# Two-layer hybrid decoder step: the MLP's down product in Strassen-Winograd form on a window of operands that moves, and low parts of weights by an accumulating DMA

## Chip, cores and metric

One NeuronCore of a Trainium2 chip runs the whole step in one launch. The metric is the device time of that launch in microseconds (us), the median of several runs.

## What is computed (the reference, cut)

Two layers over 1024 prompt tokens and 8 x 4 sample tokens, 1056 columns T in all, in fp32. The change is in the last three lines of a layer:

```python
for l in range(DEPTH):
    h = rms_norm(x, attn_norm[l])
    mix, nk, nv, ns = mixer(h, ...)          # window attention beside the HGRN2 recurrence
    x = x + jnp.einsum('ble,ed->bld', mix, w_o[l])
    h = rms_norm(x, mlp_norm[l])
    u = jnp.square(jax.nn.relu(jnp.einsum('bld,df->blf', h, w_up[l])))      # 1024 -> 4096
    x = x + jnp.einsum('blf,fd->bld', u, w_down[l])                         # 4096 -> 1024
return rms_norm(x, final_norm), ...
```

## The kernel before, in words

Activations lie transposed, features on the 128 partitions and tokens along a row. The tokens are split in `HALF` 0 (512 columns) and `HALF` 1 (544). An fp32 product is made of three matmuls in the fp32r type: each operand is split in a high part (a rounded copy) and a low part (the operand minus its high part), and `part` issues high x high, low x high and high x low into one PSUM bank. For weights `Weights.split` makes the parts: ACT copies the raw tile `wraw` into `whi`, DVE subtracts into `wlo`, 512 columns at a time; six tiles of each kind rotate. SP loads `wraw` (512 KB each, three rotate).

The up product is already in Strassen-Winograd form. Two row blocks of the weight (a pair, 16 pairs per layer) and two column blocks of the tokens of a half make a 2x2 block product that needs 7 products, not 8. `WINO` names the 7 pieces: of the weight A11, S3, S2, A12, S1, S4, A22 (the S are sums that DVE makes in place in `wraw`, or in `ws`), of the tokens B11, T3, T2, B21, T1, B22, T4. The token operands stay in SBUF for the stage, four tiles per piece and half (`x0B`, `x0T`, `x1B`, `x1T` in the traces, with high and low part in one tile). For each piece and half PE issues 4 x 3 matmuls of 256 or 272 columns; `up` then combines the 7 results out of PSUM into four blocks of u (`u11` to `u22`), which go to DRAM (`ud`).

The down product is plain: `load_u` brings a block of 128 rows of u back (`ur`), scales it by `rstd`, applies relu and square and splits it into `uh`, `ul`; `down(g)` adds four such blocks into the residual `xT`, for each of 8 output blocks, in chunks of 512, 272 and 272 columns. The last group of layer 0 loads its weights twice, to finish half 0 first; the last group of layer 1 splits its weights ahead (`split_last`), and `after` normalises as blocks end.

No engine's order is written by hand. Every operation becomes an `Op` with a modelled cost and a priority (the model's clock plus `slack[0]`), and the planner emits each engine's operations in the order that the model gives; each engine then runs its own list in that order, waiting on semaphores. PE's list comes from the generators (`up`, `down`), which yield while no PSUM bank is free in the model. PSUM has 8 banks: two of `acc`, four of `mx`, and one each for `aops` and `hops`, where the second piece's result (i = 1) of a half waits for the third.

The order of the pieces in time is:

```python
steps = [(0, h, i) for h, i in [(0, i) for i in range(6)] + [(1, 0), (1, 1), (1, 2), (0, 6)] + [
    (1, i) for i in range(3, 7)]]
steps += [(p, h, i) for p in range(1, pairs) for i in range(7) for h in range(2)]
```

Of the kernel before, what the change touches and what calls it, by code (L numbers as in the profile page):

```python
# [26 lines left out]
F32 = mybir.dt.float32  # L28
# [7 lines left out]
P = 128  # L36
# [18 lines left out]
SUMS = 20.0  # L55
LP = 2
# [14 lines left out]
TAIL = [(0, (0, 512)), (1, (0, 352)), (1, (352, 192))]  # L71
# [3 lines left out]
FG = 4  # L75
# [4 lines left out]
NG = DFF // (P * FG)  # L80
# [6 lines left out]
def tile_hybrid_step(  # L87
# [156 lines left out]

    def cols(x):
        n = 1
        for d in x.shape[1:]:
            n *= d
        return n
# [21 lines left out]
    DQ = Queue(nc.sync, None, 0.0)  # L271
    EN = dict(V=V, S=S, G=G)
# [41 lines left out]
    ud = [dram.tile([DFF // P, P, T], F32, name=f"ud{l}") for l in range(DEPTH)]  # L314
# [97 lines left out]
    class Weights:  # L412
# [4 lines left out]

        def __init__(self):
            self.src, self.raw, self.until, self.units, self.index, self.parts = [], [], [], [], {}, []
            self.last, self.s2 = 1 << 30, None  # L420
# [28 lines left out]
        def split(self, eng):  # L449
# [5 lines left out]
            def two(hi, lo, x):  # L455
                S.activation(out=hi, in_=x, func=AF.Copy)
# [26 lines left out]
        def split_last(self):  # L483
            n = UNIT // FG
            while len(self.parts) < len(self.units):
                r = self.units[len(self.parts)][2][0]
                if len(self.raw) == r:
                    self.load()
                raw, parts = self.raw[r], []
                for o in range(0, UNIT, 512):  # L490
                    hi, lo = (fresh(act.tile([P, 512], F32R, tag="A0", name="wl"), "A0", 16) for _ in range(2))
                    S.activation(out=hi, in_=raw[:, o:o + 512], func=AF.Copy)
                    (V if o else G).tensor_tensor(out=lo, in0=raw[:, o:o + 512], in1=hi.bitcast(F32), op=ALU.subtract)
                    parts += [(hi[:, c:c + n], lo[:, c:c + n]) for c in range(0, 512, n)]
                self.parts.append(parts)

        def reach(self, j, eng=V):
            while len(self.parts) <= min(j, self.last - 1, len(self.units) - 1):
# [105 lines left out]
    for l in range(DEPTH):  # L604
# [694 lines left out]
    def main():  # L1299
        xg, pre, before = [[], []], [], poolR  # L1300
        for l in range(DEPTH):
# [139 lines left out]
            us = {}  # L1441

            def load_u(f):


                tag, bufs, pool = ("A", 16, act) if (f + 8) % 14 < 8 else ("B", 12, poolU)
                us[f] = []
                slack[0] = SLACK
                for h, (base, n) in enumerate(HALF):
                    hi, lo = (fresh(pool.tile([P, n], F32R, tag=f"{tag}{h}", name=f"u{p}", bufs=bufs), f"{tag}{h}", bufs)  # L1450
                              for p in "hl")
                    r = fresh(poolU.tile([P, 544], F32, tag="ts", name="ur", bufs=3), "ts", 3)[:, :n]
                    dma(out=r, in_=ud[l][f, :, base:base + n], after=[ud[l][f, :, base + n // 2:base + n]])
                    V.scalar_tensor_tensor(out=r, in0=r, scalar=0.0, in1=rstd[h], op0=ALU.max, op1=ALU.mult)
                    S.activation(out=r, in_=r, func=AF.Square)
                    S.activation(out=hi, in_=r, func=AF.Copy)
# [258 lines left out]
```

## Time and profile before

| | |
|---|---|
| median of 3 runs | 2452.84 us (2450.91 to 2454.5) |
| profiled execution | 2449.32 us, span 2447.5 us |
| PE busy / DVE / ACT / POOL | 97% / 72% / 43% / 5% |
| mean granted TensorE clock | 0.992 |
| DMA | 256.51 MB, 105 GB/s |
| up stages | about 515 to 858 and 1735 to 2058 us |
| down stages | about 858 to 1229 and 2058 to 2434 us |

The rows below are from one profiled execution. Times are in us from the start of the span unless marked ns. "idle before" is time in which the engine did nothing ahead of an instruction, with what released it. A matmul's duration is longer than its distance to the next, since matmuls are pipelined: distances between starts are what the array takes.

### The profile page before, as it was taken

What the parts mean: (1) busy time and instruction counts of PE and PEld (TensorE: products, weight loads), DVE (VectorE), ACT (ScalarE), POOL (GpSimd) and SP (SyncE); (2) the same over time, 40 slices, a digit from 0 to 9 for tenths busy, and PEclk for the clock granted to TensorE, in tenths of its full rate; (3) what the DMA queues carried; (4) which work ended last, traced back from release to release, by engine and by line L of the source; (5) the groups of instructions that cost most, each with busy time, mean ns of one, the idle gap of its engine ahead of it and who ended that gap; (6) DMA issues with size and microseconds to landing.
All of it is one profiled execution on the core that took longest, in us unless ns stands there. A gap on an engine that the chain in (4) does not pass through costs nothing.

```text
span 2447.5 us, 43079 instructions
## 1 busy us (share of the span) xinstructions
PE 2386.2 (97%) x16752; PEld 2215.6 (91%) x16752; DVE 1768.7 (72%) x3936; ACT 1062.1 (43%) x2170; POOL 126.3 (5%) x120
## 2 busy tenths in 40 slices
PE   8999999989999999999999999999899999999997
PEld 6789998879999989999988899988899999899997
DVE  8988877896666686553688888869866667756436
ACT  6675655642222363231457556546322224523213
POOL 2000001100000000000100000101000000000003
PEclk9999999989999999999999999999999999999999
DMA  5223234423333462221322232353233335423202
GB/s 193 69 87 116 72 105 127 134 73 106 105 105 106 137 184 89 96 88 44 128 98 87 90 125 80 111 155 107 79 102 106 105 105 180 128 92 103 68 27 80
DMA packets 139468, 256.51 MB, mean 105 GB/s; under 512 B 15968, under 2 KB 73184, under 8 KB 139232
## 3 DMA queue, kind: packets, MB, share of 16 engines
q1 hardware_dynamic: 139264, 253.76, 32.0%
q8 instruction: 132, 2.16, 0.4%
q14 instruction: 72, 0.59, 0.1%
HBM read 198.37 MB, written 57.36 MB: 104 GB/s over the span
## 4 chain that ended last, share of the span: by engine, by line
PE 81%; DVE 13%; DMA 3%; ACT 2%; issue 1%; POOL 0%; SPq 0%; DVEq 0%; ACTq 0%
PE acc L347 68%; PE hops L347 3%; PE aops L347 3%; DVE wlo L231 2%; PE lv L347 2%; DMA mixL<-mixd 1%; PE sps L347 1%; PE tps L350 1%; DVE xT L231 1%; DVE z L231 1%; DMA ur<-ud 1%; DVE u L231 1%; DVE ur L231 1%; PE kv L347 1%; DVE ul L231 0%
## 5 line engine op out<-in xcount | busy, mean ns | idle before, releaser
L231 ACT ACTIVATE whi<-wraw 128x512 fp32r<-128x512 f32 x560 | 344.4, 627 | 712.8 <-PE acc L347 562.8
L231 DVE TENSOR_TENSOR wlo<-wraw,whi 128x512 fp32r<-128x512 f32 x560 | 387.0, 706 | 145.4 <-ACT whi L231 136.7
L347 PE MATMUL acc<-ul,whi 128*128 128x272 f32 (+1 forms) x1440 | 464.6, 323 | 2.3 <-DVE ul L231 2.3
L347 PE MATMUL acc<-uh,whi 128*128 128x272 f32 (+1 forms) x1440 | 464.2, 322 | 2.0 <-DVE xT L231 1.3
L347 PE MATMUL acc<-uh,wlo 128*128 128x272 f32 (+1 forms) x1440 | 463.9, 322 | 0.0
L231 DVE TENSOR_TENSOR xT<-xT,acc 128x272 f32<-128x272 f32 (+3 forms) x384 | 198.1, 518 | 261.0 <-PE acc L347 260.5
L347 PEld LDWEIGHTS acc<-uh,whi 128*128 128x128 f32 x1440 | 271.0, 188 | 23.1 <-issue 1.5
L347 PEld LDWEIGHTS acc<-ul,whi 128*128 128x128 f32 x1440 | 270.5, 188 | 22.8 <-DVE ul L231 3.2
L347 PEld LDWEIGHTS acc<-uh,wlo 128*128 128x128 f32 x1440 | 271.3, 188 | 19.7
L347 PE MATMUL acc<-xg1h,whi 128*128 128x272 f32 x704 | 214.5, 305 | 0.0
L347 PE MATMUL acc<-xg1h,wlo 128*128 128x272 f32 x704 | 202.5, 288 | 0.0
L347 PE MATMUL acc<-xg1l,whi 128*128 128x272 f32 x704 | 202.3, 287 | 0.0
L347 PE MATMUL acc<-xg0h,whi 128*128 128x512 f32 x352 | 148.0, 421 | 7.1 <-ACT xg0h L231 5.7
L347 PE MATMUL acc<-x0T,whi 128*128 128x256 f32 x768 | 142.6, 283 | 8.2 <-ACT whi L231 8.2
L347 PE MATMUL acc<-x1B,whi 128*128 128x272 f32 x768 | 148.5, 288 | 0.0
L347 PE MATMUL acc<-x1T,whi 128*128 128x272 f32 x768 | 148.2, 288 | 0.0
L347 PE MATMUL acc<-x0B,whi 128*128 128x256 f32 x768 | 142.7, 284 | 4.4 <-ACT p L231 4.4
L347 PE MATMUL acc<-xg0h,wlo 128*128 128x512 f32 x352 | 140.0, 398 | 4.4 <-DVE wlo L231 4.4
L347 PE MATMUL acc<-xg0l,whi 128*128 128x512 f32 x352 | 139.3, 396 | 1.8 <-DVE xg0l L231 1.8
L347 PEld LDWEIGHTS acc<-xg1h,whi 128*128 128x128 f32 x704 | 132.9, 189 | 3.4 <-issue 2.7
L347 PEld LDWEIGHTS acc<-xg1l,whi 128*128 128x128 f32 x704 | 132.9, 189 | 0.4
L347 PEld LDWEIGHTS acc<-xg1h,wlo 128*128 128x128 f32 x704 | 132.6, 188 | 0.0
(302 smaller groups left out, 5370.7 us busy)
## 6 DMA issues: line engine op xcount, KB each, us to landing
wraw<-win SPq DMA_DIRECT2D x86, 512.0 KB
wraw<-wd SPq DMA_DIRECT2D x68, 512.0 KB
wraw<-wu SPq DMA_DIRECT2D x64, 512.0 KB
ud<-u SPq DMA_DIRECT2D x128, 136.0 KB
ur<-ud SPq DMA_DIRECT2D x64, 272.0 KB
wraw<-wo SPq DMA_DIRECT2D x32, 512.0 KB
ud<-u SPq DMA_DIRECT2D x128, 128.0 KB
ur<-ud SPq DMA_DIRECT2D x64, 256.0 KB
```

The lines of the kernel that those rows point to most:

```text
L231: o = Op(self, ins, outs, lambda: f(*args, **kw), lambda: self.cost(op, outs[0], kw), port=shared)
L347: tensor(t, out, [lhsT, rhs], kw["start"], lambda: TE.matmul(out, lhsT, rhs, **kw))
L350: tensor(0.11, out, [in_], True, lambda: TE.transpose(out, in_, idn))
```

## The change

1. **Down in seven products.** `down` becomes the same `winograd` routine as `up`. A step p (16 per layer) makes one pair of output blocks (pair p % 4, so `xT[m]` and `xT[m+1]` with m = 2(p % 4)) from the four pairs of u blocks p to p + 3 (mod 16); the host lays `wd` out for that. The four are held in the operand tiles of the up stage. After piece i of step p has used its tiles, `load_u` loads the same piece of pair p + 4 into the slot that has come free, so the set moves by one pair a step: 19 pairs of 14 tiles are loaded per layer. Results are added to `xT` straight from PSUM.
2. **u is stored ready.** `up` now applies `rstd`, relu and square (`fin`) and makes the sums T1 to T4 of u before it stores, so `ud` holds 7 pieces of half width in place of 4 quarters, and `load_u` only splits: the DMA lands in the low part's tile, ACT copies the high part, DVE subtracts in place.
3. **Low parts by DMA.** For the pieces S3, A12, S4 of up and A11, S3, S2, A12, S4 of down, DVE's subtraction goes: ACT writes -high into `wlo`, and a DMA that POOL issues adds the raw tile to it (256 in all, 256 KB each). The planner models it as 0.8 us and 5 us more.
4. **Ends.** The sums of squares for the next norm are made as output pairs end, the two column halves of a token half get their `root` apart; `split_last`, the doubled last group, `TAIL` and `after` go.

```diff
+    class Adder(Engine):
+        def take(self, t, d):
+            return t + d, t + d + 5.0
...
+    def dma_add(out, in_):
+        Op(GQ, [in_, out], [out], lambda: nc.gpsimd.dma_start(out=out, in_=in_, accum_op=ALU.add),
+           lambda: 0.8).func = None
...
-    ud = [dram.tile([DFF // P, P, T], F32, name=f"ud{l}") for l in range(DEPTH)]
+    ud = [dram.tile([NPAIR * 7, P, T // 2], F32, name=f"ud{l}") for l in range(DEPTH)]
...
             def two(hi, lo, x):
+                if j in self.adds:
+                    S.activation(out=lo, in_=x, func=AF.Copy, scale=-1.0)
+                    dma_add(lo.bitcast(F32), x)
+                    S.activation(out=hi, in_=x, func=AF.Copy)
+                    return
                 S.activation(out=hi, in_=x, func=AF.Copy)
                 eng.tensor_tensor(out=lo, in0=x, in1=hi.bitcast(F32), op=ALU.subtract)
...
-        def split_last(self):
...
-        for p in range(NG * FG // 2):
+        for p in range(NPAIR):
             W.add_pair((l, "up", p), wu[l, 2 * p], wu[l, 2 * p + 1])
-        for g in range(NG):
-            for rep in range(2 if g == NG - 1 and l < DEPTH - 1 else 1):
-                for u in range(4):
-                    W.add((l, "down", g, rep, u), wd[l, g, u], FG)
-    W.last = W.index[DEPTH - 1, "down", NG - 1, 0, 0]
+        for p in range(NPAIR):
+            W.add_pair((l, "down", p), wd[l, p, 0], wd[l, p, 1])
+    W.adds = {i for k, i in W.index.items() if k[1]=="down" and k[-1] in (0,1,2,3,5) or k[1]=="up" and k[-1] in (1,3,5)}
...
+            def load_u(q, i, h):
+                hi, lo = operand(h, WINO[i][1])[q % 4]
+                r, o = lo.bitcast(F32), 256 * h
+                dma(out=r, in_=ud[l][7 * q + i, :, o:o + HALF[h][1] // 2])
+                S.activation(out=hi, in_=r, func=AF.Copy)
+                V.tensor_tensor(out=lo, in0=r, in1=hi.bitcast(F32), op=ALU.subtract)
...
+            def lead(p):
+                return [(p, h, i) for h, i in [(0, i) for i in range(6)] + [(1, 0), (1, 1), (1, 2), (0, 6)] + [
                     (1, i) for i in range(3, 7)]]
...
+            def winograd(phase, steps, xs, evac):
+                units = [W.index[l, phase, p, i] for p, _, i in steps]
...
+                    while phase == "up" and (i >= 3 and not rstd_ok[h] or i >= 4 and not rstd_ok[1]):
                         yield
                     slack[0] = -URGENT
+                    evac(p, h, i, acc, banks.get((h, 1)))
...
+                    def fin(t):
+                        o, x = (int(t[2]) - 1) * c, tile_(t)
+                        V.scalar_tensor_tensor(out=x, in0=x, scalar=0.0, in1=rstd[h][:, o:o + c], op0=ALU.max, op1=ALU.mult)
+                        S.activation(out=x, in_=x, func=AF.Square)
...
                         add("u12", acc, "u12")
-                        put("u12")
+                        slack[0] = LATER
+                        fin("u12")
+                        less("T3", "u22", "u12")
+                        put(1, "T3")
+                        less("u12", "u12", "u11")
+                        put(4, "u12")
+                        less("T2", "u22", "u12")
+                        put(2, "T2")
...
+                    if p == NPAIR - 1:
+                        slack[0] = SLACK
+                        for q in range(4):
+                            load_u(q, i, h)
+                yield from winograd("up", lead(0) + [(p, h, i) for p in range(1, NPAIR) for i in range(7) for h in range(2)],
...
+            def down():
+                def evac(p, h, i, acc, p7):
+                    base, n = HALF[h]
+                    c, m = n // 2, p % 4 * 2
+                    tile_, add = mine("down", p, h)
+                    def out(f, t, *ys):
+                        x = xT[m + f - 1][h][:, (t - 1) * c:t * c]
+                        for y in ys:
+                            V.tensor_tensor(out=x, in0=x, in1=y, op=ALU.add)
+                    if i == 0:
+                        S.activation(out=tile_("p1"), in_=acc, func=AF.Copy)
+                    elif i == 2:
+                        add("U2", acc, "p1")
+                        add("u21", p7, "U2")
+                    elif i == 3:
+                        out(1, 1, acc, tile_("p1"))
+                    elif i == 4:
+                        add("u12", acc, "U2")
+                        out(2, 2, acc, tile_("u21"))
+                    elif i == 5:
+                        out(1, 2, acc, tile_("u12"))
+                    elif i == 6:
+                        out(2, 1, acc, tile_("u21"))
+                    slack[0] = 3 * SLACK
+                    if p < NPAIR - 1:
+                        load_u((p + 4) % NPAIR, i, h)
...
+                yield from winograd("down", [(p, h, i) for p in range(NPAIR - 1) for i in range(7) for h in range(2)] + lead(
+                    NPAIR - 1), lambda p, h, i: [operand(h, WINO[i][1])[(p + k) % 4] for k in range(4)], evac)
...
+    wd = a["w_down"].reshape(2, 16, 2, 128, 4, 2, 128)
+    wd = np.stack([wd[:, :, :, :, s % 4][:, [(s + k) % 16 for k in range(4)]] for s in range(16)], axis=1)
+    wd = wd.transpose(0, 1, 5, 4, 3, 2, 6).reshape(2, 16, 2, 128, 1024)
```

What stands on DVE, ACT and POOL inside a step of the down stage, before and after. **DVE before**, in the down stage of layer 0 (`ur` to `uh`, `ul` is a block of u, `xT` the residual):

```order
L231 SCALAR_TENSOR_TENSOR ur<-ur,rstd_78 128x512
L231 TENSOR_TENSOR xT_0_4880<-xT_0_4880,acc 128x512
L231 SCALAR_TENSOR_TENSOR ur<-ur,rstd_79 128x544
L231 TENSOR_TENSOR xT_1_4881<-xT_1_4881,acc 128x272
L231 TENSOR_TENSOR ul<-ur,uh 128x512
L231 SCALAR_TENSOR_TENSOR ur<-ur,rstd_78 128x512
L231 TENSOR_TENSOR xT_1_4881<-xT_1_4881,acc 128x272
L231 TENSOR_TENSOR ul<-ur,uh 128x544
```

**DVE after**, from the fourth and fifth piece of a step in the middle of layer 0's down stage; the name in brackets is what the row waits for (DMAHW: an SP transfer, DMASW: a POOL transfer, with its semaphore's number):

```order
L232 TENSOR_TENSOR xT6_0_4892<-xT6_0_4892,acc_13287 128x256 [waits PE_49]
L232 TENSOR_TENSOR x1B21_6205<-x1B21_6205 128x272 [waits DMAHW1_49,Activation_49]
L232 TENSOR_TENSOR xT6_0_4892<-xT6_0_4892,u12_13262 128x256 [waits DVE_49]
L232 TENSOR_TENSOR x0T1_5492<-x0T1_5492 128x256 [waits DMAHW2_49,Activation_49]
L232 TENSOR_TENSOR xT6_1_4893<-xT6_1_4893,acc_13310 128x272 [waits PE_49]
L232 TENSOR_TENSOR wraw_12828<-ws_13242,wraw_12828 128x512 [waits DMASW0_49]
L232 TENSOR_TENSOR xT6_1_4893<-xT6_1_4893,u12_13262 128x272 [waits DVE_49]
L232 TENSOR_TENSOR x1T1_6209<-x1T1_6209 128x272 [waits DMAHW3_49,Activation_49]
L232 TENSOR_TENSOR xT7_0_4894<-xT7_0_4894,acc_13334 128x256 [waits PE_49]
L232 TENSOR_TENSOR wlo_13333<-wraw_12828,whi_13332 128x512 [waits Activation_49]
L232 TENSOR_TENSOR xT7_0_4894<-xT7_0_4894,u21_13183 128x256 [waits DVE_49]
```

The chunks of 512 and 544 columns have become pieces of 256 and 272; `wraw_12828<-ws_13242,wraw_12828` is S1, written over A11, and it waits for the POOL transfer that reads A11. Behind it on DVE stand the additions that free PSUM banks.

**ACT after**, the same step's pieces S3, S2, A12 (`wlo<-` is the negated copy), and **POOL after**, the five transfers of that step and the first of the next:

```order
L232 ACTIVATE wlo_13203<-wraw_13079 128x512 [waits DMAHW6_49,DMASW5_49,DVE_49]
L232 ACTIVATE whi_13202<-wraw_13079 128x512 [waits Activation_49]
L232 ACTIVATE wlo_13241<-ws_13242 128x512 [waits DMASW6_49,DVE_49,PE_49]
L232 ACTIVATE whi_13240<-ws_13242 128x512 [waits Activation_49]
L232 ACTIVATE wlo_13286<-wraw_12828 128x512 [waits DMASW2_49,PE_49]
L232 ACTIVATE whi_13285<-wraw_12828 128x512 [waits Activation_49]
L232 ACTIVATE x1B21_6205<-x1B21_6205 128x272 [waits DMAHW1_49]
L232 ACTIVATE x0T1_5492<-x0T1_5492 128x256 [waits DMAHW2_49]
```

```order
L288 DMA wlo_13162<-wraw_12828 128x512 [waits DMAHW3_49,DMASW4_49,Activation_49]
L288 DMA wlo_13203<-wraw_13079 128x512 [waits DMASW5_49,DMAHW6_49,PE_49,Activation_49]
L288 DMA wlo_13241<-ws_13242 128x512 [waits DMASW6_49,DMASW2_49,Activation_49]
L288 DMA wlo_13286<-wraw_12828 128x512 [waits DMASW3_49,Activation_49]
L288 DMA wlo_13373<-wraw_12828 128x512 [waits PE_49,Activation_49]
L288 DMA wlo_13456<-wraw_13123 128x512 [waits DMAHW3_49,DMASW1_49,Activation_49]
```

POOL had no instruction here before; each of its rows now waits for ACT's negated copy, and the later ones stand behind it in POOL's list.

**DVE after, where up ends**: rows of the last up pair, with loads of down's operands (`x0B`, `x1B`, `x0T`) between the additions of up (`U`, `u`):

```order
L232 TENSOR_TENSOR x0B_5456<-x0B_5456 128x256
L232 TENSOR_TENSOR u_10667<-aops,U_10666 128x256
L232 TENSOR_TENSOR U_10666<-acc,p_10580 128x272
L232 TENSOR_TENSOR x0B_5457<-x0B_5457 128x256
L232 TENSOR_TENSOR u_10667<-hops,U_10666 128x272
L232 TENSOR_TENSOR x0B_5458<-x0B_5458 128x256
L232 TENSOR_TENSOR x1B_5673<-x1B_5673 128x272
L232 TENSOR_TENSOR u_10716<-acc,p_10580 128x256
L232 TENSOR_TENSOR x1B_5674<-x1B_5674 128x272
L232 TENSOR_TENSOR x1B_5675<-x1B_5675 128x272
```

Between the addition `U_10666<-acc,p_10580` of the last up pair and its like in the first down step there are 87 rows on DVE now (82 of 256 or 272 columns, 5 of 512); an ordinary up pair has 38 (25 before), an ordinary down step 42.

## Rows read from the trace of the kernel before

**Rows 1.** The profile's page: the span; busy time, share and instructions of each engine (PE is matmul, PEld weight load); then TensorE's granted clock, in tenths of full speed, in 40 slices of the span.

```profile
span 2447.5 us, 43079 instructions
PE 2386.2 (97%) x16752; PEld 2215.6 (91%) x16752; DVE 1768.7 (72%) x3936; ACT 1062.1 (43%) x2170; POOL 126.3 (5%) x120
...
PEclk9999999989999999999999999999999999999999
```

**Rows 2.** The table of stretches, one line for each stage: up and down of layer 0, then of layer 1. Columns: the stretch in us; its length; busy us and instructions of PE, PEld, DVE, ACT, POOL; granted clock; busy share of the DMA engines; GB/s.

```profile
515.00:858.00 343.00, 335.29 (x2697) 333.53 (x2696) 227.57 (x453) 99.55 (x183) 0.00 (x0) 0.99 0.32 107
858.00:1186.00 328.00, 326.36 (x2032) 297.36 (x2032) 194.21 (x345) 106.75 (x173) 0.00 (x0) 1.00 0.31 96
1735.00:2062.00 327.00, 325.05 (x2639) 323.79 (x2640) 214.55 (x421) 90.92 (x162) 0.00 (x0) 1.00 0.34 113
2062.00:2388.00 326.00, 324.11 (x2021) 295.49 (x2021) 188.77 (x336) 103.76 (x169) 4.23 (x3) 1.00 0.29 90
```

**Rows 3.** The chain of work that ended last, in order of time: start, duration, engine, tile. One link of the up stage is 144 matmuls of one pair of blocks.

```profile
678.93 17.63 PE acc L347 x144
843.41 4.40 PE acc L347 x36
856.89 3.85 DMA ur<-ud
1776.57 17.62 PE acc L347 x144
2043.77 2.96 PE acc L347 x24
```

**Rows 4.** The timeline of PE, single matmuls (start us, duration us, shape): first of the down stage and first of the layer after it; then first and last of the down stage of layer 1.

```profile
857.95 0.40 PE L347 MATMUL acc<-uh,whi 128*128 128x512 f32 x1
1229.00 0.40 PE L347 MATMUL acc<-xg0h,whi 128*128 128x512 f32 x1
2058.29 0.40 PE L347 MATMUL acc<-uh,whi 128*128 128x512 f32 x1
2433.28 0.27 PE L347 MATMUL acc<-uh,wl 128*128 128x192 f32 x1
```

**Rows 5.** The timeline of PE in the up stage: the first of 12 matmuls on 256 columns, the first of the 12 on 272 columns behind them, and the first of the next 256.

```profile
705.22 0.40 PE L347 MATMUL acc<-x0T,whi 128*128 128x256 f32 x2
706.65 0.41 PE L347 MATMUL acc<-x1T,whi 128*128 128x272 f32 x2
708.16 0.40 PE L347 MATMUL acc<-x0B,whi 128*128 128x256 f32 x2
```

**Rows 6.** The timeline of DVE in the up stage, instructions with no idle time between them.

```profile
700.97 0.42 DVE L231 TENSOR_TENSOR U<-acc,p 128x256 f32<-128x256 f32 x1 [0.15 <-PE acc L347]
701.43 0.42 DVE L231 TENSOR_TENSOR u<-aops,U 128x256 f32<-128x256 f32 x1
...
703.31 0.68 DVE L231 TENSOR_TENSOR wlo<-wraw,whi 128x512 fp32r<-128x512 f32 x1
703.91 0.42 DVE L231 TENSOR_TENSOR u<-acc,p 128x256 f32<-128x256 f32 x1
704.26 0.68 DVE L231 TENSOR_TENSOR ws<-wraw 128x512 f32<-128x512 f32 x1
...
708.72 0.43 DVE L231 TENSOR_TENSOR u<-acc,u 128x272 f32<-128x272 f32 x1
709.07 0.68 DVE L231 TENSOR_TENSOR wlo<-wraw,whi 128x512 fp32r<-128x512 f32 x1
```

**Rows 7.** The table of stretches again, inside the up and the down stage of layer 0 away from their ends (columns as in rows 2).

```profile
560.00:800.00 240.00, 240.00 (x1963) 240.00 (x1962) 150.04 (x293) 59.68 (x106) 0.00 (x0) 1.00 0.32 104
870.00:1180.00 310.00, 309.89 (x1938) 283.11 (x1937) 180.80 (x323) 98.99 (x161) 0.00 (x0) 1.00 0.29 92
```

**Rows 8.** The page's part on DMA queues: packets, MB, share of the span of 16 engines.

```profile
q1 hardware_dynamic: 139264, 253.76, 32.0%
```

**Rows 9.** Groups of instructions, shapes kept apart: line, engine, operation, out<-in, count | busy us, mean ns of one | idle before, releaser.

```profile
L231 DVE TENSOR_TENSOR wlo<-wraw,whi 128x512 fp32r<-128x512 f32 x560 | 387.0, 706 | 145.4 <-ACT whi L231 136.7
L231 ACT ACTIVATE whi<-wraw 128x512 fp32r<-128x512 f32 x560 | 344.4, 627 | 712.8 <-PE acc L347 562.8 <-DVE wraw L231 83.9 <-issue 56.0
L231 DVE SCALAR_TENSOR_TENSOR ur<-ur,rstd 128x544 f32<-128x544 f32 x64 | 46.2, 722 | 5.1 <-DMA ur<-ud 4.7
L231 DVE TENSOR_TENSOR u<-acc,u 128x272 f32<-128x272 f32 x96 | 42.1, 438 | 27.1 <-PE acc L347 27.1
L231 DVE TENSOR_TENSOR u<-acc,u 128x256 f32<-128x256 f32 x96 | 40.3, 421 | 5.2
L231 POOL TENSOR_TENSOR u<-u,u 128x512 f32<-128x512 f32 x12 | 16.6, 1385 | 728.6 <-ACT u L231 728.6
L231 ACT ACTIVATE p<-acc 128x256 f32<-128x256 f32 x32 | 12.4, 387 | 28.9 <-PE acc L347 27.1 <-DVE x1T L231 1.9
```

**Rows 10.** The timelines of DVE and POOL after the last down matmul, when both scale the output.

```profile
2434.72 4.64 DVE L231 SCALAR_TENSOR_TENSOR y<-xT,fn_t,rstd 128x352 f32<-128x352 f32 x5
2440.76 2.82 DVE L231 SCALAR_TENSOR_TENSOR y<-xT,fn_t,rstd 128x192 f32<-128x192 f32 x5
2434.73 3.26 POOL L231 TENSOR_TENSOR y<-xT,rstd 128x352 f32<-128x352 f32 x3 [3.40 <-ACT tmp L231]
2440.80 1.91 POOL L231 TENSOR_TENSOR y<-xT,rstd 128x192 f32<-128x192 f32 x3 [2.81 <-DVE rstd L231]
```

**Rows 11.** What writes or reads the scratch tensor `ud` (SPq is SP's DMA queue; issue ns min/median/max), and who waited for it.

```profile
L278 SPq DMA_DIRECT2D ud<-u x256: 319/320/473, 534.1 to 2059.2; - x128
L278 SPq DMA_DIRECT2D ur<-ud x128: 319/320/1347, 839.3 to 2298.3; - x128
...
who waited for it (us, times):
  DVE ur L231: 12.4, 22
```

More of the change, by code (lines that the diff above doesn't have):

```diff
@@ L481, in split @@
             slack[0] = 0.0
-        def split_last(self):
[L484 to L495, printed above, removed]
         def reach(self, j, eng=V):
-            while len(self.parts) <= min(j, self.last - 1, len(self.units) - 1):
+            while len(self.parts) <= min(j, len(self.units) - 1):
                 while len(self.raw) <= self.units[len(self.parts)][2][-1]:
@@ L1439, in main @@
             yield from o_proj(1)
[L1441 to L1456, printed above, removed]
-                    V.tensor_tensor(out=lo, in0=r, in1=hi.bitcast(F32), op=ALU.subtract)
-                    us[f].append((hi, lo))
-                slack[0] = 0.0
@@ L1461, in up @@
-            def up():
-                pairs = NG * FG // 2
-                steps = [(0, h, i) for h, i in [(0, i) for i in range(6)] + [(1, 0), (1, 1), (1, 2), (0, 6)] + [
+            def load_u(q, i, h):
[4 more added lines that the diff above has]
+                V.tensor_tensor(out=lo, in0=r, in1=hi.bitcast(F32), op=ALU.subtract)
@@ L1464, in up @@
+            def lead(p):
+                return [(p, h, i) for h, i in [(0, i) for i in range(6)] + [(1, 0), (1, 1), (1, 2), (0, 6)] + [
                     (1, i) for i in range(3, 7)]]
-                steps += [(p, h, i) for p in range(1, pairs) for i in range(7) for h in range(2)]
-                units = [W.index[l, "up", p, i] for p, _, i in steps]
-                banks, tiles = {}, {}
+            def winograd(phase, steps, xs, evac):
+                units = [W.index[l, phase, p, i] for p, _, i in steps]
+                banks = {}
@@ L1502, in up @@
                         add("U2", acc, "p1")
[L1503 removed]
+                        add("u21", p7, "U2")
                     elif i == 3:
                         add("u11", acc, "p1")
[L1506 removed]
+                        slack[0] = LATER
+                        fin("u11")
+                        put(0, "u11")
                     elif i == 4:
@@ new lines, in main, with square @@
+            ssq, roots = {}, [0, 0]
+            def square(h, m, o, n, last=False):
+                x = xT[m][h][:, o:o + n]
+                if last:
+                    S.activation(out=rstd[h][:, o:o + n], in_=x, func=AF.Square)
+                    spawn(root(h, o, n))
+                elif not m:
+                    rstd_ok[h] = False
+                    ssq[h] = utile("u22" if h else "u11")
+                    S.activation(out=ssq[h][:, o:o + n], in_=x, func=AF.Square)
+                else:
+                    t = fresh(poolU.tile([P, 544], F32, tag="ts", name="sq", bufs=3), "ts", 3)[:, :n]
+                    S.activation(out=t, in_=x, func=AF.Square)
+                    V.tensor_tensor(out=ssq[h][:, o:o + n], in0=ssq[h][:, o:o + n], in1=t, op=ALU.add)
+                if l == DEPTH - 1 and m % 3 == 1:
+                    S.activation(out=x, in_=x, func=AF.Identity, scale=fn_t[:, m:m + 1])
@@ L1592, in main @@
             yield from up()
-            wide[0] = True
-            for g in range(NG):
-                yield from down(g)
-            wide[0] = False
+            yield from down()
             if l < DEPTH - 1:
```

166 lines of the change are left out of this document (78 added, 88 removed).

## The prediction

> **What bounds the kernel now.** I began with the page's busy times: PE works 97% of the span and TensorE's granted clock is at full speed in nearly all 40 slices [rows 1], so time can only come from fewer or cheaper matmuls. The table of stretches says the same by stage: in both up and both down stages PE's busy time is within a few us of the length, save the first 40 us of an up stage, and DVE, the next busiest, is at 58 to 66% [rows 2]. The chain of waits then gives the pace of the up stage, the model for what down is to become: links of a pair of blocks start at 678.93 and, eight pairs later, at 843.41, so a pair takes 20.56 us; in layer 1 it is (2043.77 - 1776.57) / 13 = 20.55 [rows 3]. Single matmuls explain the pace: 12 on 256 columns take 706.65 - 705.22 = 1.43 us and 12 on 272 take 1.51 [rows 5], and 7 x (1.43 + 1.51) = 20.6. No pair of the steady stage waits for anything. The down stage goes from 857.95 to 1229.00 = 371.1 us in layer 0, and from 2058.29 to the end of its last matmul, 2433.55, = 375.3 us in layer 1 [rows 4], 746.4 in all.
>
> **What the seven products take away.** After the change a step of down is the same 7 x 2 x 12 matmuls on the same shapes as a pair of up, with one weight piece for each 24 of them. Were PE never to wait, 32 steps would take 32 x 20.56 = 657.9 us: **88.5 us less**. That is the ceiling; everything that follows takes from it.
>
> **Is DVE still faster than PE?** In a steady up pair DVE's rows go from 25 (11 of 512 columns, 14 of 256 or 272) to 38 (8 and 30), and a down step has 42 (6 and 36). Back to back, a 512 row takes 703.91 - 703.31 = 0.60 us and a 256 row 704.26 - 703.91 = 0.35, a 272 row 709.07 - 708.72 = 0.35; one that needs the result before it takes 701.43 - 700.97 = 0.46 [rows 6]. That gives 8 x 0.60 + 30 x 0.35 = 15.3 us for up and 6 x 0.60 + 36 x 0.35 = 16.2 for down. By the mean durations, which overlap, it would be 30 x 0.43 + 8 x 0.706 = 18.5 and 36 x 0.43 + 6 x 0.706 = 19.7 [rows 9]. Before, 25 rows came to 150.04 us in 240, or 12.85 a pair [rows 7], 1.12 times what the distances give (11.5); with that factor I take 17.1 and 18.1 of 20.56. DVE stays hidden, with 2.5 us to spare in down, and no longer with 8. ACT is far off: in down 12 rows of 512 and 16 small ones, 12 x 0.63 + 16 x 0.39 = 13.8 us [rows 9].
>
> **What the accumulating DMAs cost.** They show nowhere in the trace of before. Their bytes must pass the 16 DMA engines. The main queue moved 253.76 MB in 32.0% of the span, 324 GB/s while busy [rows 8]; 104 GB/s at a share of 0.32 in the up stage says 325 [rows 7]. A down step moves two raw tiles (1.05 MB) and 14 loads (1.89 MB), 2.94 MB or 9.1 us; an up pair as much, with stores for loads. An added tile of 0.26 MB costs 0.8 us if it passes once, 1.6 if source and destination are both read, 2.4 if it passes three times. For five adds that is 13.1, 17.2 or 21.2 us a step. I take the middle, since an add reads two streams where the plain transfers of the row read one: 84% of the step, hidden, but with queues. The upper end is 0.6 us over PE's pace, 20 us in 32 steps. Between 0 and 20 I take **+10** for steady waits of both stages.
>
> The waits that they add stand in order. DVE waits for the transfer of A11 ahead of S1 and for that of A12 ahead of S4, since both sums overwrite what the transfer reads; behind them on DVE stand the additions that free PSUM, and PE waits for these when its banks are full. Six banks of 1.47 us give it some 8 us. SP waits for the adds before it reloads `wraw`, and behind that stand the loads of u; POOL's adds wait for ACT's copy and for each other. Six weight tiles rotate, each for 2.94 us of matmuls, so an add has some 10 us before PE wants it. All this is hidden while an add lands within about 8 us; beyond that each us late is a us for PE, in every step.
>
> The Trainium skill bears on this (SBUF — State Buffer, Who interferes with whom): a DVE instruction with two SBUF inputs and a GpSimd one that reads SBUF exclude each other, while a POOL-issued DMA is starved only by DVE's two-port copies. The trace agrees with the first half: beside POOL's scaling, five 352-column rows of DVE take 4.64 us, 0.93 each, where a 544-column row takes 0.72 alone [rows 9, 10]. By the second half issuing the adds would cost DVE nothing, as in my sum; no run here shows it yet.
>
> **Where up ends.** The four first pairs for down can be loaded only as the last up pair lets go of its tiles. Between the like rows of the two stages DVE has 87 rows, 82 x 0.35 + 5 x 0.60 = 31.7 us against 20.56. SP has 72 transfers there: 56 loads (7.57 MB), 14 stores (1.89), two raw tiles (1.05), 10.5 MB or 32 us, with some eight adds 39 to 45 us, in the 36 us from the first tile let go to the last one wanted. SP's issue time, 72 x 0.32 = 23 us [rows 11], isn't the limit. DVE is 11 us late, and banks and later slack of 2.5 us a step absorb part; DMA is 3 to 9 us late, of the same delay. From 1 to 15 us a layer I take 7, **+14**. Today the same place costs 1 to 3 us, already counted in the 746.4.
>
> **The smaller ends.** In the first up pair `fin` and the differences add 16 rows to DVE (5.6 us) and three subtractions go (1.8), in a stretch where DVE and `rstd` already hold PE; half of it shows: 2 a layer, **+4** (0 to 8). At the end of layer 0 the operands for the next layer need 8 x 0.64 us of DVE, less than the four pieces of half 1 that PE still has (6 us): hidden, **+1** with the tail of layer 1. There the last matmul now ends with two dependent additions, a square, a root and eight scalings of 272 columns in place of 192; before, 13.9 us pass from the last matmul to the end [rows 4, 10], and I expect 12 to 16.
>
> **Sum.** -88.5 + 10 + 14 + 4 + 1 = -59.5. The profiled execution took 2449.32 us, 3.5 below the median 2452.84 of the three runs; from the median the forecast is **2393 us**. With every cost at its lower bound it is 2364, with every one at its upper (20 + 30 + 8 + 4) 2427.
>
> **Rivals.**
> *The adds are slow.* If an add holds all 16 engines longer than (20.56 - 9.1) / 5 = 2.3 us, DMA sets the pace of down, and each us more costs 5 x 32 = 160 us. At 2.67 us the gain is gone; at 3 us the kernel takes about 2500. For it: nothing in the trace bounds an add from above. Against: three passes would be 2.4. The skill's fixed price (DMA: Bandwidth & Descriptors, Anatomy of one DMA: 2.0 us plus bytes at 436 GB/s) makes 2.6 us from issue to landing for 256 KB, by which an add would be early enough; it speaks of plain transfers, and no run here shows one from POOL.
> *POOL's issue blocks DVE.* All DVE rows between SBUF tiles have two inputs. An issue of 0.32 us, like SP's [rows 11], would cost DVE 1.6 us a step and stay hidden; one like a POOL row, 1.39 us [rows 9], would make 18.1 + 6.9 = 25 us. At 0.85 it is 22.3, 1.8 over PE, 57 us in down: about 2450, no change. The skill's rule above speaks against it.
> *DVE's list sets the pace.* With rows that wait for transfers, for ACT and for each other, 18.1 us can become 22: 1.5 x 32 = 46 us, 2439, still faster. For it: the spare is 2.5 us, and DVE runs its list in the planner's order.
>
> **Chances.** The forecast (2364 to 2427) 0.60; DVE's list 0.15; slow adds 0.12; POOL's lock 0.10, half of it slower; the rest 0.03. The range 2364 to 2450 leaves out the slow adds, half of the lock and a little below. About 0.2%, 5 us, is what a measurement here can tell from no change. Faster 0.77, same 0.05, slower 0.18.
>
> **What would show it.** Right: links of 20.56 us in the chain of both down stages; DVE busy some 85% of them; gaps of PE at the first down steps of 5 to 10 us, before matmuls on down's operands, released by DVE or by a load; DMA share about 0.8 in down. Wrong: DVE rows on `wraw` or matmuls on `wlo` that wait for POOL's transfers in every step (slow adds); DVE rows of 0.6 us or more on 256 columns (the lock); steps of 21 to 23 us with DVE never idle (its list); a lower granted clock in down.

## The result, and the profile after

The changed kernel takes 2484.84 us (median of 4 runs, 2479.80 to 2486.59), the kernel before beside it 2452.89: ratio 1.0129, 95% interval 1.0113 to 1.0145. It is 32 us **slower**; the forecast was 2393. The profiled execution took 2479.80 us, its span is 2478.0.

The page of the changed kernel (answers to [rows 1, 8]): span, busy times, granted clock in 40 slices, the two DMA queues that carry data, the group of POOL's issues, and the issue with its median us to landing.

```profile
span 2478.0 us, 49266 instructions
PE 2347.5 (95%) x17534; PEld 2223.2 (90%) x17534; DVE 2007.3 (81%) x5027; ACT 1369.9 (55%) x3106; POOL 330.0 (13%) x361
...
PEclk9999999989999989999999999999899998999998
...
q1 hardware_dynamic: 225472, 314.95, 41.1%
q0 software_dynamic: 36864, 67.13, 15.3%
...
L288 POOL DMA_DIRECT2D wlo<-wraw x224 | 194.6, 880 | 1210.0 <-ACT wlo L232 756.3
...
wlo<-wraw POOLq DMA_DIRECT2D x224, 256.0 KB, 4.5
```

PE works less than before (2347.5 against 2386.2 us) and waits more. DVE is not full. The stretches of the changed kernel (columns as in [rows 2]): up away from its ends, the end of up, the first down step, down away from its ends; then the first down step and the later ones of layer 1.

```profile
600.00:840.00 240.00, 238.83 (x1941) 237.61 (x1940) 186.34 (x439) 107.96 (x231) 30.51 (x35) 1.00 0.66 178
845.00:865.00 20.00, 17.41 (x137) 16.65 (x136) 13.84 (x40) 12.45 (x32) 2.40 (x3) 1.00 0.95 278
865.00:905.00 40.00, 26.88 (x170) 25.73 (x169) 30.50 (x81) 24.64 (x64) 4.52 (x6) 0.79 0.95 259
910.00:1180.00 270.00, 259.47 (x2079) 255.36 (x2078) 206.99 (x519) 151.25 (x347) 53.73 (x62) 1.00 0.82 200
2084.00:2122.00 38.00, 27.07 (x164) 25.72 (x164) 29.79 (x81) 24.05 (x63) 4.33 (x5) 0.78 0.93 257
2125.00:2400.00 275.00, 260.87 (x2063) 255.46 (x2062) 207.53 (x518) 152.62 (x352) 53.03 (x62) 0.99 0.79 191
```

Two things stand out against [rows 7]: the first down step has PE busy for 27 of 40 us, at a granted clock of 0.79 (part of it at 1.2 GHz, behind waits), with the DMA engines at 0.95; and the later steps have PE idle for 10.5 of 270 us while DVE is busy for 77%. The waits of PE in that first step (in brackets: idle before, and what ended it):

```profile
871.54 0.80 PE L357 MATMUL aops<-x0T,whi 128*128 128x256 f32 x2 [3.34 <-ACT whi L232]
876.44 0.58 PE L357 MATMUL aops<-x0T,wlo 128*128 128x256 f32 x1 [4.10 <-DMA wlo<-wraw]
890.65 0.50 PE L357 MATMUL acc<-x0T,whi 128*128 128x256 f32 x2 [3.43 <-ACT whi L232]
...
897.99 0.58 PE L357 MATMUL acc<-x0B,wlo 128*128 128x256 f32 x1 [2.04 <-DMA wlo<-wraw]
```

Two of them are waits for an added tile itself, 6.1 us (6.5 in layer 1). In all later steps of both layers such waits come to 3.1 us.

A pair of up and a step of down are each 168 matmuls, so a step is measured from the first matmul of one to the first of the next, in the profiled execution. The first three boundaries of layer 0's down stage, on PE's timeline (start, duration, shape): steps of 40.24 and 23.91 us.

```profile
865.11 0.40 PE L357 MATMUL acc<-x0B,whi 128*128 128x256 f32 x2
...
905.35 0.50 PE L357 MATMUL acc<-x0B,whi 128*128 128x256 f32 x2
...
929.26 0.40 PE L357 MATMUL acc<-x0B,whi 128*128 128x256 f32 x2
```

All runs in one table, each cell layer 0 / layer 1 in us: mean of pairs 2 to 15 of up; last pair of up and first step of down together (PE alone needs 41.1); mean of steps 3 to 13 of down; the down stage; and the time as a ratio to the kernel before, with its interval; four kernels ran once, and their time stands there instead.

| kernel | up pair | last + first | down step | down stage | ratio |
|---|---|---|---|---|---|
| before | 20.56 / 20.55 | | | 371.1 / 375.3 | 1 |
| changed | 20.79 / 20.81 | 64.4 / 65.8 | 21.77 / 22.37 | 373.5 / 374.3 | 1.0129 (1.0113 to 1.0145) |
| e1 no adds in down | 20.56 / 20.91 | 59.6 / 59.4 | 21.04 / 21.15 | 355.8 / 354.7 | 0.9962 (0.9948 to 0.9975) |
| e2 none in first step | 20.88 / 20.86 | 60.4 / 61.0 | 22.26 / 21.89 | 378.2 / 371.0 | 1.0120 (1.0104 to 1.0136) |
| e3 S4 over A21 | 20.83 / 20.63 | 66.6 / 65.9 | 21.63 / 21.77 | 371.3 / 368.5 | 1.0101 (1.0075 to 1.0126) |
| e4 no adds | 21.00 / 20.99 | 58.3 / 57.0 | 21.16 / 21.19 | 355.9 / 354.8 | 0.9956 (0.9939 to 0.9973) |
| e5 traffic in layer 1 | 20.96 / 20.85 | 61.0 / 69.8 | 21.02 / 22.37 | 356.0 / 376.7 | 2468.09 us, one run |
| e6 two sets | 20.81 / 20.82 | 59.8 / 63.0 | 21.86 / 20.94 | 366.1 / 355.7 | 2455.49 us, one run |
| e7 POOL issues | 21.05 / 20.86 | 60.0 / 59.1 | 21.18 / 20.96 | 353.7 / 348.3 | 0.9968 (0.9958 to 0.9977) |
| e8 half raw tiles | 20.56 / 20.55 | 68.4 / 69.8 | 20.68 / 20.94 | 365.1 / 361.2 | 1.0027 (1.0018 to 1.0037) |
| e9 u loads later | 21.01 / 20.91 | 57.6 / 66.4 | 20.94 / 21.04 | 351.4 / 359.1 | 0.9978 (0.9966 to 0.9991) |
| e10 halves, fewer adds | 20.56 / 20.55 | 60.1 / 58.1 | 20.98 / 20.92 | 359.3 / 352.5 | 0.9926 (0.9911 to 0.9941) |
| e11 e10, u later | 20.56 / 20.55 | 55.4 / 64.6 | 21.01 / 21.08 | 353.7 / 362.2 | 0.9948 (0.9933 to 0.9962) |
| e12 halves, no adds | 20.56 / 20.55 | 60.9 / 57.6 | 21.41 / 21.17 | 362.4 / 354.4 | 0.9928 (0.9912 to 0.9943) |
| e13 traffic or wait | 20.75 / 20.88 | 58.2 / 69.1 | 21.48 / 22.45 | 357.1 / 378.2 | 2468.32 us, one run |
| e14 transition | 20.89 / 20.74 | 51.5 / 52.8 | 21.00 / 21.02 | 344.1 / 348.6 | 2420.77 us, one run |
| e15 together | 20.56 / 20.55 | 56.4 / 54.7 | 21.02 / 20.85 | 357.2 / 350.5 | 0.9934 (0.9920 to 0.9947) |

Stretches with the same program differ here by up to 0.5 us in the mean up pair (layer 0 of e1, e7) and by 1.4 us in "last + first" (layer 0 of e1, e5); differences of that size carry nothing. The layers differ too: in the changed kernel a step of layer 1 is 0.6 us longer than one of layer 0, so layer 1 is compared with layer 1.

**Where a late step comes from.** One stall of 2.08 us in layer 0, on the timelines of SP, POOL, ACT, DVE and PE:

```profile
1085.88 0.33 SPq L284 DMA_DIRECT2D wraw<-wd  x1
...
1087.48 0.33 SPq L284 DMA_DIRECT2D wraw<-wd  x1
1087.90 0.38 SPq L284 DMA_DIRECT2D x1T<-ud  x1
1087.51 0.87 POOL L288 DMA_DIRECT2D wlo<-wraw  x1 [2.43 <-ACT x0T L232]
...
1095.51 0.43 ACT L232 ACTIVATE x1T<-x1T 128x272 fp32r<-128x272 f32 x1 [4.57 <-DMA x1T<-ud]
...
1094.80 0.69 DVE L232 TENSOR_TENSOR wraw<-wraw 128x512 f32<-128x512 f32 x1 [2.16 <-DMA wraw<-wd]
...
1097.16 0.50 PE L357 MATMUL acc<-x0B,whi 128*128 128x256 f32 x2 [2.08 <-DVE xT L232]
```

Both raw tiles of a pair come free within 1.6 us and are reloaded together; an add starts at the same moment (and lands 8.6 us later, the longest of the 256). The load of u issued behind them at 1087.90 lets ACT go on only at 1095.51, and DVE gets the raw tile at 1094.80. ACT and DVE run their lists in order, so the additions that free PSUM stand behind, and PE waits. Between 910 and 1180 us ACT's waits say the same, in the changed kernel and then in e1 (total, times, longest):

```profile
ACT x1T L232 <- DMA x1T<-ud: 53.7, 22, 4.6
ACT x0T L232 <- DMA x0T<-ud: 15.4, 15, 3.5
```

```profile
ACT x1T L232 <- DMA x1T<-ud: 19.5, 10, 3.0
ACT x0B L232 <- DMA x0B<-ud: 19.2, 18, 2.7
```

Over all four kinds of tile ACT waits 86.6 us for loads of u there, in e1 49.6.

### The profile page after: what moved, and what is told of

Its sections match the earlier page's. It is cut to its first block, busy times and chain, and to the rows that moved or that the text cites. A ratio compares the mean times of both kernels' runs of the same rounds, so it can differ in the third digit from the quotient of the medians.

```text
span 2478.0 us, 49266 instructions
## 1 busy us (share of the span) xinstructions
PE 2347.5 (95%) x17534; PEld 2223.2 (90%) x17534; DVE 2007.3 (81%) x5027; ACT 1369.9 (55%) x3106; POOL 330.0 (13%) x361
## 3 DMA queue, kind: packets, MB, share of 16 engines
q1 hardware_dynamic: 225472, 314.95, 41.1%
q0 software_dynamic: 36864, 67.13, 15.3%
## 5 line engine op out<-in xcount | busy, mean ns | idle before, releaser
L288 POOL DMA_DIRECT2D wlo<-wraw x224 | 194.6, 880 | 1210.0 <-ACT wlo L232 756.3
L357 PE MATMUL acc<-x0B,whi 128*128 128x256 f32 x1536 | 291.8, 288 | 23.2 <-ACT p L232 12.2
L357 PE MATMUL acc<-x1B,whi 128*128 128x272 f32 x1536 | 302.7, 293 | 6.9 <-DVE U L232 3.6
L357 PEld LDWEIGHTS acc<-x0B,whi 128*128 128x128 f32 x1536 | 242.3, 193 | 29.4 <-ACT p L232 12.7
L357 PEld LDWEIGHTS acc<-x0T,whi 128*128 128x128 f32 x1536 | 241.3, 192 | 26.8 <-DVE xT L232 11.7
L357 PEld LDWEIGHTS acc<-x1B,whi 128*128 128x128 f32 x1536 | 244.3, 192 | 10.5 <-DVE u L232 5.9
L357 PEld LDWEIGHTS acc<-x1T,whi 128*128 128x128 f32 x1536 | 242.6, 191 | 10.5 <-DVE xT L232 6.7
L357 PE MATMUL acc<-x0T,wlo 128*128 128x256 f32 x768 | 219.8, 286 | 5.2 <-DVE wlo L232 3.9
L357 PE MATMUL acc<-x0B,wlo 128*128 128x256 f32 x768 | 219.9, 286 | 4.4 <-DMA wlo<-wraw 4.4
L357 PE MATMUL acc<-x1B,wlo 128*128 128x272 f32 x768 | 223.2, 291 | 0.0
L357 PE MATMUL acc<-x1T,wlo 128*128 128x272 f32 x768 | 222.9, 290 | 0.0
```

The costliest lines, as they stand in the source:

```text
L288: Op(GQ, [in_, out], [out], lambda: nc.gpsimd.dma_start(out=out, in_=in_, accum_op=ALU.add), lambda: 0.8).func = None
L357: tensor(t, out, [lhsT, rhs], kw["start"], lambda: TE.matmul(out, lhsT, rhs, **kw))
```

## Experiments

The planner writes new lists for every kernel, so a difference also holds what that moved.

**e1 and e4: take the adds away.**
```diff
-W.adds = {... "down" and k[-1] in (0,1,2,3,5) or "up" and k[-1] in (1,3,5)}
+W.adds = {... "up" and k[-1] in (1,3,5)}        # e1;   e4: set()
```


> The five added low parts of each down step go back to DVE (up keeps its three); all else as in the changed kernel. Theory A (the adds and what waits behind them are late: DVE's sums wait for an add, the reload of wraw waits for it, the first down matmuls wait for it): DVE's list grows by 5 x 0.60 = 3.0 us to about 19.8 us a step, still under 20.56, so steady down steps fall from 22.2 to about 20.8 (30 x 1.4 = 42 us) and the first step of each layer by 8 (16 us): about 2425 us. Rival B (DVE's list with its own waits sets the pace): 16.8 + 3.0 us plus the present 5.4 us of waits make steps of 24 to 25 us, about 2550 us.

> No accumulating DMA at all: up and down make every low part on DVE, as the kernel before does in up; Strassen's form in down stays. Theory A: down as in the run without down's adds, and the steady up pairs go back from 20.8 and the like to 20.56, 14 us in all: about 2412 us. Rival B: DVE has 38 + 11 rows there, 17.1 + 1.8 us in up, which stays under the pace, so up gains no more than 3 us and down is at 24 to 25 us a step: about 2545 us.


Without down's adds the kernel is faster than before by 0.38%; the down stages take 37 us less in all, with DVE busy 19.6 us a step (steps 3 to 13, 93%). So the adds cost more than the DVE work that they save. Up's adds do nothing measurable for the whole. The direction is theory A's, the size is not: 2439 in place of 2425, since steps are at 21.1, not 20.8, and the transition from up to down (last pair and first step) keeps 18 us a layer too many.

**e2 and e3: undo single waits for an add.**
```diff
+W.adds: "down" and k[2] > 0 ...                      # e2
-combine(a12, a12, self.s2)                           # e3
+combine(a21, a12, self.s2)                           # and S4=a21 in two(...)
```


> Only the first down step of each layer makes its low parts on DVE. Theory A: in that step PE no longer waits 4.1 + 2.0 us (layer 0) and 4.5 + 2.0 us (layer 1) for an added tile, and the matmuls at half clock behind these waits become fewer: 8 us a layer, about 2468 us. Rival D (the 56 loads of u and their copies on ACT and DVE hold the first step, the add is only the last to come): the waits are taken over by ACT's copies, less than 2 us a layer, 2481 to 2485 us.

> S4 is written into the tile half of A21, which is no longer needed, and not over A12: DVE's sum then does not wait for A12's add, and the first raw tile comes free without S4's copy and add. Same number of instructions and bytes. Theory A: the reload of wraw starts some 6 us earlier, the steady steps of down fall from 22.2 to about 21.2: 30 us less, about 2455 us, up's last 8 us of steady waits with them. Rival C (the 16 DMA engines are too busy at 0.7 to 0.8, transfers are slow whatever waits for them): within 6 us of the changed kernel, 2479 to 2488 us.


Both gain little, and less than theory A asked. In e2 PE waits for ACT's weight copies in the first step (9.9 us in layer 0) where it waited for added tiles; the last pair and first step get 4 to 5 us shorter, but the second step takes 26.7 and 26.6 us in place of 23.9 and 23.4. In e3 steps fall by 0.1 and 0.6 us. SP's own waits tell why A is weak in the steady stage: of the changed kernel between 930 and 1170 us, only the last line is an add's (total, times, longest).

```profile
SPq L284 <- PE acc L357: 136.6, 128, 3.4
SPq L284 <- DVE x1T L232: 19.3, 11, 3.0
...
SPq L284 <- DMA wlo<-wraw: 3.8, 7, 1.2
```

**e5 and e13: the transfers without the waiting.**
```diff
+Op(GQ, ..., lambda: nc.gpsimd.dma_start(out=amask[:, :512], in_=carry.rearrange(...), accum_op=ALU.add))
```


> As the run without down's adds, but in layer 1's down stage POOL also issues five accumulating DMAs of 256 KB a step, from a tile that nobody writes into a tile that nobody else reads (amask, no longer needed): the transfers without anything that waits for them. Layer 0's down stage has none and is the control; without them the two stages took 355.8 and 354.7 us. Theory A (it is the waits for the adds): layer 1's down stage stays within 5 us, 355 to 360 us. Rival C (the transfers themselves slow the loads of wraw and u): it comes near the changed kernel's 374, at least 365 us.

> The changed kernel's lists, but down's adds are left out: in layer 0 nothing takes their place, so the low parts stay at minus the high copy; in layer 1 POOL issues, after ACT's copy, an accumulating DMA of the same size from carry into amask, which nobody waits for. DVE's list is the changed kernel's in both. With adds the down stages took 373.5 and 374.3 us. Theory A (waiting for the adds costs): both layers fall alike, steady steps 20.6 to 20.8, stages of 350 us or less. Theory C (their traffic, which delays the loads of u and of wraw): layer 0 falls to 350 us or less, layer 1 stays above 362 us.


Traffic that nobody waits for makes a loss as large as the whole: layer 1's stage takes 376.7 us in e5, against 354.7 in e1 and 374.3 in the changed kernel. Between e1 and e5 nothing differs but that traffic: the rows of PE, DVE, ACT and SP are the same and stand in the same order. In e13, layer 1's stage takes 378.2 us. ACT's waits for loads of u between 2110 and 2380 us go from 51.8 us in e1 to 70.9 in e5. The steady stretches of layer 0 and layer 1 of e5, with layer 1 of e1 behind them, then those of e13:

```profile
910.00:1180.00 270.00, 268.44 (x2154) 264.88 (x2153) 252.08 (x617) 128.43 (x302) 0.00 (x0) 1.00 0.48 148
2110.00:2380.00 270.00, 259.36 (x2046) 253.50 (x2045) 238.86 (x584) 122.19 (x285) 48.56 (x56) 0.99 0.76 187
...
2110.00:2380.00 270.00, 267.46 (x2144) 263.72 (x2143) 251.54 (x614) 130.79 (x306) 0.00 (x0) 1.00 0.46 141
```

```profile
910.00:1180.00 270.00, 264.93 (x2107) 259.54 (x2106) 212.50 (x534) 154.80 (x358) 0.00 (x0) 1.00 0.46 143
2110.00:2380.00 270.00, 255.07 (x1999) 249.38 (x1999) 202.28 (x507) 147.31 (x339) 48.83 (x57) 0.99 0.76 186
```

Theory A falls and C is borne out, with one point off: e13's layer 0 has neither traffic nor waits and DVE at 79%, and still takes 21.48 us a step, not 20.8, only 0.3 less than with the adds; its stage is 16.4 us shorter, mostly in the first two steps and the last ones. DVE waits there 32 us in 270 for one copy of ACT (`x1B`), but e8 below has nearly the same wait (26.5) and steps of 20.68. The rows on DVE and ACT are the changed kernel's, but their order isn't, against what was expected. So 0.5 to 0.9 us a step stay without any add in down; whether the order of the lists makes them, or loads that are late by themselves, isn't shown.

**e6: which adds.**
```diff
+W.adds: "down" and k[-1] in ((0,2), (1,3,5))[k[0]] ...
```


> Down's adds split over the layers: layer 0 has those of A11 and S2, layer 1 those of S3, A12 and S4; up keeps its three. Without adds in down the stages took 355.8 and 354.7 us, with all five 373.5 and 374.3. Theory A: A11's add is waited for only by S1 four pieces later and S2's reads ws, so layer 0's stage comes to 356 to 360 us; S3's, A12's and S4's hold both raw tiles and DVE's S4, so layer 1's comes to 366 to 372. Rival C (traffic by count): 2 of 5 and 3 of 5 of the loss, 363 and 366 us.


The reverse of A, and not C by count: three adds (S3, A12, S4) cost nothing in layer 1's steady steps, two (A11, S2) cost 0.8 us a step in layer 0. Why those two hurt more wasn't settled: ACT waits for loads of u alike in both (62 and 66 us in 270), and the lists differ in more than the adds.

**e8: give the reloads time.**
```diff
-RAW = 3   # tiles of 1024 columns;  until += [n + 5, n + 6]
+RAW = 6   # halves A11, A21, A22, A12; until += [n + 4, n + 5, n + 6, n + 5]
+combine(a21, a12, self.s2)   # as in e3
```


> The changed kernel with all its adds, but the raw tiles are rings of six halves of 512 columns in place of three of 1024, loaded in the order A11, A21, A22, A12, and S4 is written over A21: in the same memory each half comes free as soon as its own pieces are done, and a reload has 15 us or more before DVE wants it. Same bytes and the same DVE and PE rows, two more loads a step. Theory A (the reload of wraw behind the adds sets down's steps): steady steps fall from 22.2 to about 20.8 us, 40 us less in 30 steps, 2440 us where the kernel before has 2449 and the changed one 2481; the first steps keep their 40 us. Rival (the wait of PE for the added tile itself, or traffic): steps stay above 21.7, 2465 us or more.


With all 256 adds and the DMA engines at a share of 0.85, up pairs are at 20.56 us and 11 down steps at 20.68 and 20.94: in these steps traffic costs next to nothing where the raw tiles come in halves, each reloaded as it comes free. ACT's waits for loads of u between 910 and 1180 us fall from 86.6 us to 36.3. (Over steps 2 to 16, which hold the slower ones at both ends, e8 takes 322.1 and 317.7 us, e1 319.9 and 319.5.) The move of S4 alone, e3, gave 21.63 and 21.77. The stretch of layer 0:

```profile
910.00:1180.00 270.00, 267.34 (x2159) 265.82 (x2159) 214.89 (x543) 162.17 (x368) 56.37 (x65) 0.99 0.85 209
```

The transition gets worse, 68.4 and 69.8 us. e12 shows that halves alone do not do it: without adds steps stay at 21.2 to 21.4, with DVE busy 92% of the stretch. That DVE's fuller list is the reason is argued and not shown, since e13's layer 0 takes as long with DVE at 79%.

**e7, e9, e14: the transition from up to down.**
```diff
+if first and h: nc.gpsimd.dma_start(out=r, in_=src)      # e7, on e1
+slack[0] = (3 * SLACK, 6 * SLACK)[l]                      # e9, on e1, for the first load_u
+if not (first and l == 1 and not h): dma(...)            # e14, on e1: 28 loads left out
+if first and l == 0: return                               # e14: 56 differences left out
```


> As the run without down's adds, but POOL issues the 28 loads of half 1 for the four first pairs of each down stage, which SP issued, 0.48 us apart, in a row of 98 transfers. Theory S (SP's issuing, 98 x 0.486 = 48 us, holds the transition): the last up pair and the first down step fall from 23.7 + 35.9 and 24.2 + 35.2 us by about 8 us a layer: 16 us less, 2423 against 2439 with the kernel before at 2449. Rival (DVE's 31 us of rows in the first step and DMA's 0.80 to 0.86 hold it): 4 us a layer or less.

> As the run without down's adds; the loads of the four first pairs of each down stage, with their copies and differences, get a lower priority in the planner (clock + 18 in layer 0, + 36 in layer 1, in place of + 6), so that ACT's list has the weights' copies ahead of copies that wait for a load. Theory O (ACT's order: PE's waits for whi, 8.1 and 6.1 us of the first step, are whi copies queued behind x copies whose loads land late): last up pair and first step fall from 59.6 and 59.4 us to about 53 in a layer or both, 2427 us with the kernel before at 2449. Rival (the loads themselves and DVE's 31 us set it): the wait for whi turns into one for the operands, 58 us or more, 2437 to 2443.

> The run without down's adds; for the four first pairs of down, layer 0 leaves out DVE's 56 differences (the low parts stay the raw values) and layer 1 leaves out the 28 loads of half 0 (the tiles keep old values). Without either, last up pair and first step took 59.6 and 59.4 us, where PE alone needs 41.1. Theory V (DVE's 31 us of rows set it): layer 0 falls to 50 us or less, layer 1 by less than 3 us. Theory M (the loads set it, 0.80 to 0.86 of the DMA engines at 242 to 268 GB/s): layer 1 falls to 52 us or less, layer 0 by less than 3 us.


SP issues almost without a pause from 840.92 to 888.56 us in e1 (87 transfers; the 98 of the expectation was a miscount), but a second issuer gains nothing: issuing isn't the limit. The order counts: with the loads' priority 18 later, last pair and first step get 2 us shorter in e9, near the noise, and 3.4 to 4.7 in e11 and e15; with 36 later they get 7 us longer. e14 splits the rest: without DVE's 56 differences (layer 0) 8.1 us go, without half of the loads (layer 1) 6.6, of 18. So neither V nor M holds alone: taking away either shortens the place. That the two delays add up isn't shown, as no run takes away both. Last pair and first step of e14, layer 0 and layer 1:

```profile
842.30:893.90 51.60, 44.08 (x339) 43.05 (x338) 35.50 (x83) 33.59 (x88) 0.86 (x1) 0.97 0.88 271
2028.10:2081.00 52.90, 45.53 (x339) 44.07 (x338) 49.99 (x134) 34.79 (x96) 0.87 (x1) 0.94 0.70 217
```

**e10 to e12, e15: what beats both kernels.**
```diff
+W.adds: "down" and k[2] > 1 ... or "up" and k[2] < NPAIR - 1 ...   # e10, on e8
+slack[0] = (3 * SLACK, 6 * SLACK)[l]                               # e11;  e15: 3 * SLACK in both
```


> The run with half raw tiles, but without adds in the last up pair and the first two down steps of each layer. Theory C (the adds' traffic, beside 56 loads, lengthens the transition): last up pair and first step fall from 68.3 and 69.8 us to the 59.5 of the run without down's adds, the other steps stay at 20.6 to 20.9: 17 us less, about 2438 us with the kernel before at 2449. Rival (the half tiles themselves lengthen it, 64 transfers more on SP): 66 us or more, no gain.

> The run above with the lower priority for the first loads of u as well. If theory O holds the two gains add up: 53 us for last pair and first step, about 2425 us; if not, as the run above, 2436 to 2441.

> Half raw tiles and S4 over A21, and no accumulating DMA at all. Without adds and with whole tiles steady steps took 20.9 to 21.1 us of 19.2 us DVE work. If the late raw tiles alone made that difference from 20.56, they fall to 20.6: 12 us less, about 2427 us; if it is DVE's list with its waits (19.2 + 1.4 us), they stay at 20.9 to 21.1, 2436 to 2442 us.

> Half raw tiles, S4 over A21, no adds in the last up pair and the first two down steps, and the first loads of u at clock + 18 in both layers. The run with + 6 took 60.1 and 58.1 us for last up pair and first step, and 0.9926 of the kernel before; with + 18 in layer 0 alone 55.4 there. If that holds in layer 1 too, 4 us a layer: about 2423 us with the kernel before at 2449, ratio 0.990; if the order in layer 1 falls out differently, 2431 us.


e10 does what C said: the transition goes from 69 to 59 us without its adds. It is 0.74% faster than the kernel before (2431.12 against 2448.54 us). e15's transition is 3.5 us shorter, but the first step with adds then takes 23.2 us, so e10, e12 and e15 can't be told apart. e12 has no add at all: even with the half tiles the adds earn nothing that shows.

## Why the prediction was wrong

By its terms, in us of the span (2478.0 - 2447.5 = 30.5; the measured ones add up to 30.7), each as forecast and as measured (the forecast's upper end adds up to 2426, not 2427):

| term | forecast | measured |
|---|---|---|
| 32 steps at PE's pace | -88.5 | -88.5 (taken over; undisturbed steps, as in e5 and e8, take 20.54 to 20.56) |
| steady waits, up and down | +10 | 6.8 in up, 52.1 in down's 30 later steps |
| up to down, both layers | +14 | 64.4 + 65.8 - 2 x 41.1 = +48.0 |
| first up pair | +4 | 35.52 - 34.76 + 36.72 - 33.17 = +4.3 |
| ends | +1 | +8 |

- **The ceiling** and **DVE's price** were right. DVE is busy 16.8 us in a down step (forecast 18.1) and 31 in the first (31.7). Without adds it is 19.6, still less than PE's pace.
- **The adds' bytes** were right too. The share in down is 0.82 (forecast 0.84); the adds bring it from 0.48 to 0.82, which is 0.34 x 22 / 5 = 1.5 us (a step is some 22 us long) of all engines for each (forecast 1.6); POOL's queue by itself says the same, 15.3% of 2478.0 us for 256 adds. They land 4.5 us after the issue in the median, and only one of the 256 later than the 8 us that the text allowed.
- **The step that failed** is the next sentence: "All this is hidden while an add lands within about 8 us". It asked when an add would be late, and not what its traffic does to the other loads. A load of u or of a raw tile that arrives beside an add and another raw tile holds ACT's and DVE's lists, and behind them PE's banks; such traffic alone, with nothing waiting for it, made layer 1's stage 22 us longer (e5 against e1). Of the 52.1 us, 29.4 go when down's adds go, although DVE's list grows: steps 2 to 16 take 333.2 and 335.6 us with them, 319.9 and 319.5 in e1. The other 22.7 stay in e1; whether DVE's fuller list or loads that are late by themselves make them is open. A busy share averaged over a step shows nothing of this.
- **The transition** was mis-sized: the text took DVE's 11 us and DMA's 3 to 9 as one delay ("of the same delay"), partly absorbed by slack. It measured 48 us, not 14. In e14 taking away DVE's differences or half of the loads is worth 7 to 8 us by itself; 36.8 of the 48 stay without adds. The DMA rate taken was 324 GB/s while busy [rows 8]; here the engines moved 257 to 278 GB/s at a share of 0.93 to 0.95, 273 to 293 while busy, and in e1, without the adds, 254 at 0.84, which is 302.
- **The ends**: the last matmul ends at 2458.15, 19.9 us before the end (forecast 12 to 16). The stretch between the layers is 2.4 us longer.
- **The rivals**: none of the three was it. An add holds the engines for 1.5 us, not 2.3; DVE's list is at 77%. POOL's issue takes 880 ns, and DVE's rows are no longer than before: those of 256 columns still take 0.42 us [rows 9]. The rule of the Trainium skill (SBUF — State Buffer, Who interferes with whom) that was cited, by which issuing on POOL costs DVE nothing, agrees with these 0.42 us. Of the signs named, a lower granted clock came in the first down steps, behind waits. Waits for POOL's transfers came in few places, not in every step: DVE rows on `wraw` waited 3.5 us in all, matmuls on `wlo` 15.7, of which 12.6 in the two first down steps.

## What to carry to other kernels

A DMA that nobody waits for isn't free: price it by what else is in the queues when it runs, load by load, and ask how long before its use each load is issued, since an average share of 0.8 says nothing about that. Moving work from an engine to DMA can pay only where the loads have lead time: smaller tiles that come free one by one made the same traffic nearly harmless in the steady steps, in the same memory, though even there it bought nothing (e10 against e12). Where two stages meet, don't take the delays of two resources for one unless a run shows it: here taking away either shortened the place.

## What the runs showed of the hardware

An accumulating DMA of 256 KB inside SBUF costs 1.5 us of all 16 engines and lands 3.8 to 4.6 us (median) after its issue, which takes POOL 0.88 us. 80 such adds that nobody waits for made layer 1's down stage 22 us longer (e5 against e1), at a mean share of the DMA engines of 0.76. In the changed kernel's first down step PE waited four times for 2.0 to 4.1 us; the granted clock of the stretch was 0.79, as part of it ran at 1.2 GHz behind these waits (a matmul of 256 columns took 0.58 us there and 0.28 elsewhere). The waits are 13 us of the 19.7 that this step takes beyond 20.56.
